# Moving attention's preparation beside the samples' columns, and the heads' sums of squares into the next unit

## The chip, the cores and the metric

The kernel runs on one core of a Trainium2 chip (trn2). The metric is the device time of one execution in microseconds. Of the kernel before there are three timed runs and one profiled execution.

## What is computed

The reference is one inference step of a hybrid decoder trunk: a prompt of 512 tokens behind 16 meta tokens, and 8 sample tokens with caches. Cut to what matters:

```python
xn = rmsnorm(x, norm_gain)
h = jnp.einsum('btd,de->bte', xn, w_in)                       # 2048 -> 16 q heads, 4 k, 4 v, z_a, u, z_s, g_a, g_s
q, k, v, z_a, u, z_s, g_a, g_s = jnp.split(h, IN_SPLITS, axis=-1)
q = rope(rmsnorm(q.reshape(b, t, 16, 64), q_norm_gain), pos)  # per head of 64
k = rope(rmsnorm(k.reshape(b, t, 4, 64), k_norm_gain), pos)
...
s = einsum(q, k) / 8                                          # window of 128, 16 meta keys, one sink per head
w = exp(s - m) / (sum(exp(s - m)) + exp(sink - m))
o = einsum(w, v)                                              # times the gate of z_a, then a 2048-wide merge
```

Beside attention stands a branch of 64 diagonal state-space groups on u, and both are merged by gates and two more products with weights. The sample tokens attend to 128 cached keys, 16 meta keys and themselves.

## The kernel before

**Columns.** The 528 prompt positions and 8 sample tokens are 536 columns, in two halves c of CH = 268; the last four columns of each half are samples. Activations have features on the partitions and columns on the free axis.

**Units.** Every weight block of 128 output rows is a unit. The fp32 weights come from HBM by SP (`raw`, L1006), ScalarE casts a high part (`whi`, L1007), VectorE subtracts it for a low part (`wlo`, L1008), three buffers each. `mm` (L1164) multiplies a unit: two weight tiles (h = 0, 1), eight k-tiles each, three products of high and low parts, two column halves, so 96 matmuls of 260 or 268 columns into one PSUM tile of the pool `mmp`, which has two buffers. VectorE frees it by the product `z<-mm` with the columns' norms R: L1194 in `evac` for gate blocks, with tanh (L1199) and L1200 behind it, and L1325 in `heads`. Later stages (L1373) form other groups of products out of the same weights.

**Order of the units.** ORDER1 writes it out by hand: "xuhuhuhuhuhuhuhuhhhhh", where x is a gate block, u an input of the state-space branch, h one of twelve head blocks: keys (0, 1), values (2, 3), queries (4 to 11). Gate blocks and later products follow.

**Head blocks.** `heads(i)` evacuates the block, stores it in DRAM twice, straight and with the halves of each head swapped (`rawD`), and squares it on ScalarE. After every odd i other than 3 four matmuls with the selector `sel` (L1343) sum the squares of two blocks per head; ScalarE copies them out (L1346), and SP stores them to `skD` (keys) or `sqD` (queries). After i = 11 `head_norms` (L1353) loads all sums back in a compact form (L1357), scales them (L1358), takes reciprocal roots by three Newton steps on VectorE (`rsqrt_dve`, L559 to L564), and stores `rkD` and `rqD` (L1360). `z` and `t` in these steps are rings of two buffers that the evacuations use as well.

**The background.** `Background` holds generators in lanes. Out of `mm`, every `grain` k-tiles, it is stepped with a budget: a generator's `yield cost` uses credit, `yield None` ends its lane's turn until the next step. `samples()` (lane 2) prepares the sample columns: loads of the heads' columns and their norms (`x<-rawD`, `x<-rkD`, `x<-rqD`, by GpSimd, L576 to L583), rope on VectorE (L588 to L593), two transposes on TensorE (L597, L598), copies (L602, L603), stores, and then the sample attention itself. `attention()` (lane 0) waits until `smp` is filled, which happens once those copies and stores of the samples are issued. Then it loads its constants (`k_attc`, L1106) and, in this order, makes the values (`vb`, `mt`, L758 to L776, with transposes on TensorE), the keys (loads `sbw<-rawD` L697 and `rb<-rkD` L701; rope L712, L713, L715; product with the norms L724; `out_k` L734; high part KH L747, low part KL L749; copies to the other partitions L752), the first q (`load_q`, then rope L712 to L715, L721, high and low parts `QT` L788, L789), and the scores (L805, L806), softmax, transposes and weighing, block by block for four kv heads. The pool of `sbw`, `sv` and `rb` has two buffers.

**What sets the order on the engines.** A tile framework places the instructions of the program by a simulated timeline and priorities; evacuations and weight splits have a high one (HIGH). On each engine the instructions then stand in a fixed row, and one that waits holds all behind it.

## Time and profile before

| | |
|---|---|
| three runs | 1272.38, 1271.10, 1270.46 us |
| median | 1271.1 us |
| profiled execution | 1273.38 us |
| its span, first to last instruction | 1271.6 us |
| mean granted TensorE clock in it | 0.995 |
| DMA traffic in it | 219.22 MB, 172 GB/s |

In the rows of the profile PE is TensorE, PEld its weight loads, DVE is VectorE, ACT ScalarE, POOL GpSimd, SP the engine that issues most DMAs; a q behind a name is its sequencer. `mm<-xh,whi` means: written is mm, read are xh and whi. A timeline row has the start, the duration, engine, line, operation, tiles, shape and count, and in brackets how long the engine had stood idle before it and what ended that. PEclk is the granted TensorE clock, 1.00 being full speed.

### The profile page before, as it was taken

The page shows a single profiled execution, that of the slowest core. Times are in us where ns is not written, and L with a number is a line of the kernel's source. Part 1 is how long each engine was busy: PE and PEld are TensorE (multiplying, and loading weights), DVE is VectorE, ACT ScalarE, POOL GpSimd, SP SyncE. Part 2 cuts the span into 40 slices and gives each one's busy share as a digit, 9 for nine tenths or more (in the row PEclk, how much of TensorE's full clock was granted, in tenths as well). Part 3 has the DMA queues.
Part 4 walks back from the last instruction along what each step waited for, and adds up shares of the span by engine and source line. Part 5 has one row for each costly group of instructions (what it writes and reads, how often), then busy time and mean ns, then how long its engine had stood idle before and what let it go on. Part 6 is the DMA issues. An engine that isn't in the chain of part 4 may idle for free.

```text
span 1271.6 us, 26531 instructions
## 1 busy us (share of the span) xinstructions
PE 1254.8 (99%) x10357; PEld 1230.1 (97%) x10357; DVE 980.0 (77%) x1554; ACT 629.2 (49%) x1344; POOL 264.2 (21%) x437
## 2 busy tenths in 40 slices
PE   9999999999999998999999998999999999999998
PEld 9999999999999998999999998999999999999998
DVE  8686888887787567888798277999976467787775
ACT  8554444454545594556523234567556333344342
POOL 0003999940000141222220133110011000000000
PEclk9999999999999998999999998999999999999999
DMA  8544343353434654555554767777666665565441
GB/s 293 203 157 157 123 142 128 123 177 129 146 109 154 223 171 138 169 164 165 152 149 129 232 170 224 220 261 222 206 196 239 195 191 183 157 204 157 146 141 51
DMA packets 108002, 219.22 MB, mean 172 GB/s; under 512 B 21933, under 2 KB 47493, under 8 KB 107845
## 3 DMA queue, kind: packets, MB, share of 16 engines
q1 hardware_dynamic: 99172, 198.53, 49.0%
q0 software_dynamic: 8704, 19.00, 5.7%
q8 instruction: 81, 1.33, 0.4%
q14 instruction: 45, 0.36, 0.1%
HBM read 181.57 MB, written 36.82 MB: 172 GB/s over the span
## 4 chain that ended last, share of the span: by engine, by line
PE 81%; DMA 7%; DVE 4%; ACT 4%; issue 2%; SPq 1%; POOL 0%; DVEq 0%; POOLq 0%; ACTq 0%
PE mm L1164 37%; PE pr L1373 35%; ACT ct L346 2%; PE wg L854 2%; DMA raw<-in_w 2%; PE aux L1373 1%; DMA c<-in_cT 1%; DVE wlo L1008 1%; DMA xr<-in_x 1%; PE aux L805 1%; ACT whi L1007 1%; DMA x<-rawD 1%; DMA bN<-in_bN 1%; PE aux L806 1%; PE mm L1680 1%
## 5 line engine op out<-in xcount | busy, mean ns | idle before, releaser
L1074 DVE TENSOR_TENSOR wlo<-raw,whi 128x1024 fp32r<-128x1024 f32 x161 | 198.7, 1256 | 69.5 <-ACT whi L1073 69.2
L1073 ACT CAST whi<-raw 128x1024 fp32r<-128x1024 f32 x161 | 166.5, 1049 | 167.7 <-DVE raw L1072 76.0
L1007 ACT CAST whi<-raw 128x1024 fp32r<-128x1024 f32 (+3 forms) x128 | 122.3, 965 | 141.6 <-PE mm L1164 95.4
L1164 PE MATMUL mm<-xh,whi 128*128 128x260 f32 (+1 forms) x792 | 186.4, 289 | 0.2 <-ACT xr L1222 0.2
L1164 PE MATMUL mm<-xl,whi 128*128 128x260 f32 (+1 forms) x792 | 184.6, 286 | 0.0
L1164 PE MATMUL mm<-xh,wlo 128*128 128x260 f32 (+1 forms) x792 | 184.6, 287 | 0.0
L1008 DVE TENSOR_TENSOR wlo<-raw,whi 128x1024 fp32r<-128x1024 f32 (+3 forms) x128 | 142.2, 1119 | 45.6 <-ACT whi L1007 44.9
L1373 PE MATMUL pr<-tau,whi 128*128 128x260 f32 x928 | 168.6, 283 | 0.0
L1373 PE MATMUL pr<-cb,whi 128*128 128x260 f32 x848 | 153.0, 283 | 0.0
L1373 PEld LDWEIGHTS pr<-tau,whi 128*128 128x128 f32 x928 | 143.0, 188 | 0.0
L1164 PEld LDWEIGHTS mm<-xh,whi 128*128 128x128 f32 x792 | 133.1, 190 | 3.4 <-issue 2.6
L1164 PEld LDWEIGHTS mm<-xl,whi 128*128 128x128 f32 x792 | 133.5, 190 | 0.8 <-issue 0.8
L1164 PEld LDWEIGHTS mm<-xh,wlo 128*128 128x128 f32 x792 | 132.4, 190 | 0.0
L1373 PEld LDWEIGHTS pr<-cb,whi 128*128 128x128 f32 x848 | 130.8, 188 | 0.2 <-ACT z L1407 0.2
L1373 PE MATMUL pr<-tau,wlo 128*128 128x260 f32 x464 | 130.8, 282 | 0.0
L1373 PE MATMUL pr<-cb,wlo 128*128 128x260 f32 x424 | 119.1, 283 | 0.2 <-DVE wlo L1074 0.2
L1072 DVE TENSOR_TENSOR raw<-raw 128x1024 f32<-128x1024 f32 x91 | 113.1, 1243 | 1.6
L1164 PE MATMUL mm<-Y,whi 128*128 128x260 f32 x576 | 104.7, 287 | 0.0
L1373 PE MATMUL pr<-xl,whi 128*128 128x260 f32 x352 | 98.9, 283 | 0.0
L1373 PE MATMUL pr<-xh,wlo 128*128 128x260 f32 x352 | 98.8, 283 | 0.0
L1373 PE MATMUL pr<-xh,whi 128*128 128x260 f32 x352 | 97.1, 283 | 0.0
L1373 PEld LDWEIGHTS pr<-tau,wlo 128*128 128x128 f32 x464 | 87.2, 188 | 0.0
(421 smaller groups left out, 2980.2 us busy)
## 6 DMA issues: line engine op xcount, KB each, us to landing
raw<-in_w SPq DMA_DIRECT2D x202, 512.0 KB, 4.6
gD<-z SPq DMA_DIRECT2D x34, 260.0 KB, 3.1
t<-gD SPq DMA_DIRECT2D x32, 260.0 KB, 2.9
cache<-in_vc POOLq DMA_DIRECT2D x16, 286.0 KB, 3.6
cache<-in_kc POOLq DMA_DIRECT2D x15, 288.0 KB, 4.1
xr<-in_x SPq DMA_DIRECT2D x16, 268.0 KB, 6.5
xg<-in_x SPq DMA_DIRECT2D x8, 536.0 KB, 4.6
sbw<-rawD SPq DMA_DIRECT2D x16, 260.0 KB, 4.3
```

Of the source, the lines that this page charges most:

```text
L346: nc.scalar.activation(out=dst, in_=src, func=AF.Copy, scale=x)
L805: nc.tensor.matmul(ps[:, e, 0:272], lhsT=q, rhs=KH[:, k0:k0 + 272], start=True, stop=False)
L806: nc.tensor.matmul(ps[:, e, 0:272], lhsT=q, rhs=KL[:, k0:k0 + 272], start=False, stop=True)
L854: nc.tensor.matmul(pv[64 * e:64 * e + 64, 0:256], lhsT=V, rhs=pr[:, e::2], start=(i == 0), stop=(i == len(parts) - 1))
L1007: nc.scalar.copy(out=hi, in_=raw)
L1008: self.dve = nc.vector.tensor_tensor(out=lo, in0=raw, in1=hi.bitcast(F32), op=ALU.subtract).ins
L1072: nc.vector.tensor_tensor(out=o, in0=o, in1=i, op=ALU.add)
L1073: nc.scalar.copy(out=hi, in_=t)
L1074: nc.vector.tensor_tensor(out=lo, in0=t, in1=hi.bitcast(F32), op=ALU.subtract)
L1164: m = nc.tensor.matmul(ps[:, c, 0:W], lhsT=wt[:, k], rhs=xo(kt, c), start=f, stop=l)
L1373: m = nc.tensor.matmul(bank, lhsT=wt[:, p], rhs=x(p, e), start=first and f and p == 0, stop=l and p == 7, skip_group_check=not first and l ...
L1680: nc.tensor.matmul(ps[:, c, 0:260], lhsT=w2[kt // 8][j][:, kt % 8], rhs=xk(xh, kt, c, 8), start=False, stop=(kt, j) == (15, 1))
```

## The change

The counts of instructions are the same on TensorE; what changes is when things are issued.

- The sums of squares of `heads` become a function that is put on a list `pend`. `mm` calls all that is on it when the first half (h = 0) of the unit's products has been issued, so the sums of a pair stand in the middle of the next unit.
- `head_norms`, the start of `samples()` and a mark in `normed` go on the same list after the last head block.
- `attention()` starts on that mark, no longer on `smp`. Its values, keys and first q no longer wait for the samples' columns.
- Before the first q's rope it passes NLOAD = 3 steps, and after it waits for `smp`, so that the first scores are issued behind the samples' transposes, copies and stores. Between the first q and its scores it passes NDELAY = 1 step, before 2.

```diff
-NDELAY = 2
+NLOAD = 3
+NDELAY = 1
...
+    pend, normed = [], []
+
     def mm(n, hi_of, lo_of, w0, budget=None, after=None, pool=None, name=None):
...
+            while pend and h == 0:
+                pend.pop(0)()
             if after:
                 after(h)
...
-        if i % 2:
+        def sums():
             if "ax" not in S:
                 S["ax"] = aux.tile([P, 2, 512], F32, name="aux")
             ps = S["ax"][:, 1, P:]
...
+        if i % 2:
+            pend.append(sums)
...
             if n == 11:
-                head_norms()
-                bg.add(samples(), lane=2)
+                pend.extend((head_norms, lambda: bg.add(samples(), lane=2), lambda: normed.append(1)))
             continue
...
-        while not smp:
+        while not normed:
             yield None
...
         for kv in range(4):
+            if kv == 0:
+                for _ in range(NLOAD):
+                    yield None
             yield from at.queries(kv)
+            while not smp:
+                yield None
             if kv == 0:
                 for _ in range(NDELAY):
                     yield None
```

Line numbers in the changed kernel are higher by 1 near the weights, by 6 from `evac` to `heads` and by 9 in `head_norms`.

**VectorE, the keys beside an evacuation.** Before, from the keys' rope on; L1194 is the evacuation `z<-mm`, L724 the keys' product with their norms `rb`, KL the low parts of the keys:

```order
L713 SCALAR_TENSOR_TENSOR sbw<-sbw,k_attc 128x536
L1200 SCALAR_TENSOR_TENSOR z<-t,z 128x520
L715 TENSOR_TENSOR sbw<-sbw 128x536
L1194 TENSOR_TENSOR z<-mm,R 128x520
L724 TENSOR_TENSOR sbw<-sbw,rb 128x536
L1008 TENSOR_TENSOR wlo<-raw,whi 128x1024
L715 TENSOR_TENSOR sbw<-sbw 128x536
L1200 SCALAR_TENSOR_TENSOR z<-t,z 128x520
L749 TENSOR_TENSOR KL_9463<-sbw,KH_9459 64x4x64 x2
```

In the changed kernel, where the evacuation is L1200:

```order
L1009 TENSOR_TENSOR wlo<-raw,whi 128x1024
L563 SCALAR_TENSOR_TENSOR t<-t,z 128x65
L724 TENSOR_TENSOR sbw<-sbw,rb 128x536
L564 SCALAR_TENSOR_TENSOR z<-t,z 128x65
L724 TENSOR_TENSOR sbw<-sbw,rb 128x536
L562 TENSOR_TENSOR t<-z 128x65
L749 TENSOR_TENSOR KL_9336<-sbw,KH_9332 64x4x64 x2
L1200 TENSOR_TENSOR z<-mm,R 128x520
L563 SCALAR_TENSOR_TENSOR t<-t,z 128x65
L749 TENSOR_TENSOR KL_9336<-sbw,KH_9332 64x4x16
```

Before, the evacuation stood ahead of both products L724 and of all KL; now both products and the first KL steps stand ahead of it.

**VectorE, the first q beside the next evacuation.** Before; the rows on `128x520` with `k_attc` are the first q's rope, which waits for the load `sbw<-rawD`, and x_9262 belongs to the samples:

```order
L592 TENSOR_TENSOR x_9262<-x_9262 128x64
L749 TENSOR_TENSOR KL_9466<-sbw,KH_9462 64x4x64 x2
L749 TENSOR_TENSOR KL_9466<-sbw,KH_9462 64x4x16
L712 SCALAR_TENSOR_TENSOR sbw<-sbw,k_attc 128x520
L713 SCALAR_TENSOR_TENSOR sbw<-sbw,k_attc 128x520
L715 TENSOR_TENSOR sbw<-sbw 128x520
L1194 TENSOR_TENSOR z<-mm,R 128x520
L721 TENSOR_TENSOR sbw<-sbw,rb 128x4x64 x2
L1008 TENSOR_TENSOR wlo<-raw,whi 128x1024
L1200 SCALAR_TENSOR_TENSOR z<-t,z 128x520
```

In the changed kernel, where x_9361 belongs to the samples:

```order
L593 COPY x_9361<-x_9361 128x16
L1206 SCALAR_TENSOR_TENSOR z<-t,z 128x520
L712 SCALAR_TENSOR_TENSOR sbw<-sbw,k_attc 128x520
L713 SCALAR_TENSOR_TENSOR sbw<-sbw,k_attc 128x520
L1200 TENSOR_TENSOR z<-mm,R 128x520
L591 TENSOR_TENSOR x_9361<-x_9361 128x64
L591 TENSOR_TENSOR x_9361<-x_9361 128x16
L712 SCALAR_TENSOR_TENSOR sbw<-sbw,k_attc 128x520
L713 SCALAR_TENSOR_TENSOR sbw<-sbw,k_attc 128x520
L1009 TENSOR_TENSOR wlo<-raw,whi 128x1024
```

Before and now one evacuation stands behind the first q's rope; now it is that of an earlier unit, the samples' steps are spread around it, and the second q's rope follows at once.

**SP, from the keys' norms to the first q's loads.** Before; rkD and rqD are the norms, `rb` their copies on all partitions, `sbw<-rawD` of 128x2x260 the loads of the first q:

```order
L1360 DMA rkD<-z 67x32
L701 DMA rb<-rkD 64x536 x2
L1006 DMA raw<-in_w 128x1024
L701 DMA rb<-rkD 64x536 x2
L1006 DMA raw<-in_w 128x1024
L1360 DMA rqD<-z 128x65
L1201 DMA gD<-z 128x520
L734 DMA out_k<-sbw 128x536
L701 DMA rb<-rqD 64x520 x2
L1006 DMA raw<-in_w 128x1024
L1201 DMA gD<-z 128x520
L697 DMA sbw<-rawD 128x2x260 x2
```

In the changed kernel:

```order
L1366 DMA z<-sqD 128x65
L1007 DMA raw<-in_w 128x1024
L1369 DMA rkD<-z 67x32
L701 DMA rb<-rkD 64x536 x4
L1007 DMA raw<-in_w 128x1024
L734 DMA out_k<-sbw 128x536 x2
L697 DMA sbw<-rawD 128x2x260 x2
L1369 DMA rqD<-z 128x65
L697 DMA sbw<-rawD 128x2x260 x2
L1007 DMA raw<-in_w 128x1024
L701 DMA rb<-rqD 64x520 x2
```

Ahead of the store of rkD a weight block now stands behind the load `z<-sqD`, the four `rb` of the keys stand together, and the first q's loads moved ahead of rqD, of a gate's store gD and of the q norms' `rb`.

## The prediction, made before the result was known

> **What bounds the kernel now.** I read the page's busy shares first, then TensorE's chain of waits, then 4-us windows around the waits. The page:

> ```profile
> PE 1254.8 (99%) x10357; PEld 1230.1 (97%) x10357; DVE 980.0 (77%) x1554; ACT 629.2 (49%) x1344; POOL 264.2 (21%) x437
> ```

> TensorE is busy for 99% of the span, so a change that adds and removes no matmul can gain only where TensorE waits, or where its clock is low. Its waits (microseconds in all, times, longest):

> ```profile
> PE aux L1343 <- DVE sst L486: 6.2, 2, 4.6
> PE aux L805 <- DVE QT L789: 3.9, 1, 3.9
> ```

> The change names both lines: L1343 is the heads' sums of squares, L805 the first scores. The windows (stretch, its length, busy time and instructions of PE, PEld, DVE, ACT, POOL, then PEclk, DMA share, GB/s) show what a wait costs beside its own length:

> ```profile
> core 0: us, PE busy (x) PEld busy (x) DVE busy (x) ACT busy (x) POOL busy (x), PEclk, DMA share, GB/s
> 500.00:504.00 4.00, 1.91 (x12) 1.06 (x12) 3.97 (x17) 1.44 (x3) 0.09 (x1) 0.68 0.00 0
> 624.00:628.00 4.00, 2.36 (x23) 1.73 (x22) 3.87 (x15) 4.00 (x17) 0.27 (x1) 1.00 0.44 131
> 628.00:632.00 4.00, 4.00 (x45) 3.66 (x44) 3.33 (x6) 1.98 (x4) 1.68 (x4) 1.00 0.42 143
> 764.00:768.00 4.00, 4.00 (x34) 3.84 (x33) 2.02 (x3) 0.00 (x0) 2.53 (x5) 1.00 1.09 310
> 768.00:772.00 4.00, 0.05 (x2) 0.01 (x1) 3.94 (x8) 2.88 (x4) 2.24 (x5) 0.89 0.82 227
> 772.00:776.00 4.00, 4.00 (x17) 3.78 (x18) 3.93 (x6) 0.40 (x1) 3.36 (x7) 0.50 0.91 259
> 776.00:780.00 4.00, 4.00 (x28) 4.00 (x28) 3.67 (x8) 2.50 (x4) 0.22 (x1) 0.76 1.07 341
> 800.00:825.00 25.00, 25.00 (x209) 24.19 (x208) 23.80 (x42) 15.36 (x39) 3.98 (x7) 1.00 0.77 227
> ```

> At 768 to 772 TensorE stands for 3.95 us. In the next 8 us the granted clock is 0.50 and then 0.76, and 17 + 28 = 45 matmuls are done where the undisturbed window at 764 does 34 in four. The missing 2 x 34 - 45 = 23, at 4.00/34 = 0.118 us each, are 2.7 us. The stall at the first scores therefore costs 3.95 + 2.7 = 6.65 us. The wait of 1.64 us (4.00 - 2.36 at 624) is followed by clock 1.00: it cost only itself. Between these two lies the length at which a wait begins to cost the clock too; I take the middle, 2.8 us.

> **The sums in the next unit.** The same matmuls, copies and stores are issued, so this edit adds no work. In the changed order of instructions the sums of heads 1, 5 and 7 stand exactly where they stood; only those of 9 and 11 move, by about half a unit, and no row shows TensorE waiting at those two. The 6.2 us of L1343 thus stay: gain 0, cost 0 for the sums themselves. What the edit does cost lies behind the last pair: the head norms now start behind later sums, and the work that hung on the samples is queued differently. That is a path of DMAs and VectorE steps, whose prices are these. SP's issues before:

> ```profile
> 735.67 0.33 SPq L1357 DMA_DIRECT2D z<-sqD  x1
> 736.12 0.25 SPq L1360 DMA_DIRECT2D rkD<-z  x1
> 738.05 1.18 SPq L701 DMA_DIRECT2D rb<-rkD  x2
> ...
> 755.09 1.27 SPq L697 DMA_DIRECT2D sbw<-rawD  x2
> ```

> The store of the norms in the chain that ended last, and three answers on DMAs (count, KB each, median us to landing): the keys' loads at 708 with nothing else under way, rb at 738, and the crowd of 750 to 760:

> ```profile
> 736.12 1.92 DMA rkD<-z
> ```

> ```profile
> sbw<-rawD SPq DMA_DIRECT2D x4, 268.0 KB, 6.7
> ```

> ```profile
> rb<-rkD SPq DMA_DIRECT2D x2, 134.0 KB, 3.3
> ```

> ```profile
> raw<-in_w SPq DMA_DIRECT2D x2, 512.0 KB, 11.8
> KH<-KH POOLq DMA_DIRECT2D x4, 144.0 KB, 8.1
> KL<-KL POOLq DMA_DIRECT2D x4, 144.0 KB, 8.2
> out_k<-sbw SPq DMA_DIRECT2D x2, 268.0 KB, 4.8
> rb<-rqD SPq DMA_DIRECT2D x4, 130.0 KB, 8.7
> ```

> VectorE's steps (start, duration, what it waited for), and ScalarE's cast that marks a unit's start:

> ```profile
> 746.80 0.22 DVE L564 SCALAR_TENSOR_TENSOR z<-t,z 128x65 f32<-128x65 f32 x1
> ...
> 749.48 0.71 DVE L724 TENSOR_TENSOR sbw<-sbw,rb 128x536 f32<-128x536 f32 x1
> ...
> 752.47 1.81 DVE L749 TENSOR_TENSOR KL<-sbw,KH 64x256 fp32r<-64x256 f32 x6
> ...
> 765.42 0.76 DVE L712 SCALAR_TENSOR_TENSOR sbw<-sbw,k_attc 128x520 f32<-128x520 f32 x1 [6.58 <-DMA sbw<-rawD]
> 766.71 0.76 DVE L713 SCALAR_TENSOR_TENSOR sbw<-sbw,k_attc 128x520 f32<-128x520 f32 x1 [0.53 <-DMA sbw<-rawD]
> 767.50 0.70 DVE L715 TENSOR_TENSOR sbw<-sbw 128x520 f32<-128x520 f32 x1
> 768.12 0.69 DVE L1194 TENSOR_TENSOR z<-mm,R 128x520 f32<-128x520 f32 x1
> 768.73 0.75 DVE L721 TENSOR_TENSOR sbw<-sbw,rb 128x256 f32<-128x256 f32 x2
> 769.40 1.22 DVE L1008 TENSOR_TENSOR wlo<-raw,whi 128x1024 fp32r<-128x1024 f32 x1
> 770.53 0.69 DVE L1200 SCALAR_TENSOR_TENSOR z<-t,z 128x520 f32<-128x520 f32 x1
> 771.25 1.41 DVE L789 TENSOR_TENSOR QT<-sbw,QT 64x512 fp32r<-64x512 f32 x2
> ```

> ```profile
> 747.57 1.05 ACT L1007 CAST whi<-raw 128x1024 fp32r<-128x1024 f32 x1 [1.69 <-issue]
> ```

> **What goes.** Before, the first q's rope (L712) got its load at 765.42, 10.3 us after its issue, and its QT came late for the first scores. Now the q load is issued earlier and the scores stand behind the samples' transposes, about 17 matmuls later. I take this stall as gone: 6.65 us.

> **What is late next: the evacuations.** A unit's PSUM is freed by VectorE's product z<-mm (L1194), and with two PSUM buffers each unit waits for the evacuation of the unit but one before. In the new order both evacuations of this stretch stand behind attention's steps that wait for a DMA, and all VectorE work behind those steps is queued too.

> *Stall A, keys.* Now rkD's last step stands behind the step that waits for z<-sqD. Issue 735.7 as before; 3.3 us to land (price of rb at 738, the nearest small load); two small steps of 0.2: 739.4. Store 1.9: 741.3. Four rb issues of 0.59, the last begun by 743.1 and done by 743.7; 3.3 us more: 746.4 to 747.0. Both key products L724 are ahead of the evacuation, then two small steps (0.4) and two KL steps (1.81/6 = 0.3 each): 0.7 + 0.4 + 0.6 + 0.7 for the evacuation = 2.4, so it ends at 748.8 to 749.4. TensorE is ready for that unit at about 747.4 (the cast at 747.57 stands at the same boundary). Stall A is 1.4 to 2.0; I take 2.0, since a wait's end also has to travel. The far end of rb is the crowd's 8.7, but the crowd comes later; that end I leave to the slower cases.

> *Stall B, the first q.* TensorE goes on at 749.4 and needs the next evacuation 96 matmuls later, 96 x 0.119 = 11.5: 760.9. It stands behind L712 and L713, which wait for the q loads. These use the buffer that out_k of the first keys frees: keys' product about 746.6, out_k 4.8, so issue at 751.4 and 752.0. Landing: 6.7 with nothing beside it, 8.7 like the crowd's rb, 10.3 like the same load before. I take 7.7, between the first two, because of the transfers queued on SP ahead of it only one out_k is then still under way, while the KH and KL copies are. So 759.1 and 759.7; 0.76 + 0.76 + 0.69: evacuation done at 761.3, stall B 0.4. Ends: 0 at 6.7, 1.4 at 8.7, 3.5 at 10.3 (with the second load 1.29 behind the first, as at 766.71).

> *Stall C, the samples' transposes.* From that evacuation to the samples' last product VectorE has 0.4 of small adds, 0.76 + 0.76, 1.22, 0.70, 0.2, 0.69, 0.70, 0.75, 0.69, 1.22, 0.75, 0.70, 0.2 = 9.7; rows overlap by some 0.08 each (768.12 to 768.73 is 0.61 for 0.69), fourteen times 1.1: 8.65. TensorE gets there after 65 matmuls, 7.75. Stall C 0.9, or about 0 when B leaves VectorE a lead.

> The sum: 2.0 + 0.4 + 0.9 = 3.3 added, none over 2.8, so no clock is lost; 6.65 removed; **3.35 gained**. The profiled execution took 1273.4 (span 1271.6) and would take 1270.0; the median of the runs is 1271.1, and from it the forecast is **1267.8**.

> [...]

> **The rivals.** *1, faster: the loads land as in an empty chip.* Loads at 6.7, stall A 1.4, B 0, C 0.2 at most: 1.4 to 1.6 added, 5.1 gained, 1266.0. For it: the q load comes some 4 us earlier than at 755.09. Against: the DMA share there was over 1, and eight KH/KL copies come at the same time. [...]

> *2, slower: the evacuation is held by a late q load.* From a landing of 9.6 us on B passes 2.8 and TensorE's clock falls as at 772: at 10.3, 2.0 + 3.5 + 2.7 + 0.9 = 9.1, 2.45 lost, 1273.6; at the 11.8 of raw (evacuation at 763.2 + 2.2 = 765.4, B 4.5) 10.1, 3.45 lost, 1274.6. For it: the same load did take 10.3. Against: it stood among more transfers then.

> *3, no change: the lead is given back.* VectorE has 23.80 of 25 us busy at 800; where TensorE comes earlier, VectorE's next evacuations can be late by as much: 1271.1. Against: TensorE waits nowhere there now, with 1.2 us to spare in 25.

> **How the numbers follow.** Forecast's own case 0.42 (landings 7.2 to 9.0, 1267.0 to 1269.1), rival 1 0.20, rival 2 0.24, rival 3 0.10, anything else 0.04. About 0.2%, 2.5 us, is what a measurement can tell from no change. Of the forecast's case 0.30 gains more than that and 0.12 less. Faster 0.30 + 0.20 + 0.01 = 0.51; same 0.12 + 0.10 + 0.01 = 0.23; slower 0.24 + 0.02 = 0.26. The range goes from rival 1 with rb at its best (1265.6) to rival 2 at 1274.6; the forecast's own is 1267.0 to 1269.1.

> **What would show it.** Right: the waits of the changed kernel still have L1343 with 6.2 us in two; L805 <- QT is gone; in its place mm <- z (evacuation) with about 2 and under 1.5 us, and a wait of the samples' transposes under 1; PEclk stays 1.00 from 745 to 785. Step A is wrong if the keys' rb land after 747.5, step B if L712 of the first q starts outside 758 to 761. The prediction is wrong if a 4-us window there shows PEclk 0.5, if L1343's waits change, or if TensorE waits anew between 780 and 1000.

## The result and the profile after

The changed kernel took 1263.7 us (median of 5 runs, 1260.33 to 1264.03), the kernel before 1270.46 us (5 runs, 1267.56 to 1272.38): ratio 0.9943, 95% interval 0.9928 to 0.9958, so 5 to 9 us faster. In a later series, with other runs of both, it was 0.9959 (0.9941 to 0.9976). The forecast was 1267.8, 3.35 us faster, with a range that began at 1265.6. The profiled execution of the changed kernel took 1264.03 us, its span is 1262.3.

TensorE's waits after (line waited at, engine and line waited for, us in all, times, longest):

```profile
PE mm L1168 <- DVE t L563: 2.9, 1, 2.9
PE tr L1216 <- DVE var L1270: 1.1, 1, 1.1
...
PE aux L1349 <- DVE sst L486: 0.6, 1, 0.6
```

The first scores (L805) have left the list, as forecast, and an evacuation (`mm` waits) has come in with 2.9 us, as forecast, if longer. (The list names L563, a small step that stands right behind the evacuation L1200 in VectorE's row; L1200 ran from 740.57 to 741.25, and TensorE went on at 741.40.) But the sums of squares (L1349, before L1343), which were to keep 6.2 us, have 0.6. The windows show the same at their two places, the sums at 496 to 504 and the evacuation at 736 to 748:

```profile
496.00:500.00 4.00, 4.00 (x36) 3.42 (x36) 3.15 (x6) 3.80 (x13) 0.56 (x1) 1.00 0.23 92
500.00:504.00 4.00, 4.00 (x44) 3.66 (x43) 4.00 (x13) 0.67 (x3) 3.83 (x8) 1.00 0.54 150
```

```profile
736.00:740.00 4.00, 2.46 (x21) 2.25 (x19) 1.73 (x5) 1.83 (x7) 0.71 (x2) 1.00 0.80 252
740.00:744.00 4.00, 2.60 (x12) 2.63 (x13) 3.91 (x14) 3.17 (x8) 2.61 (x6) 0.57 0.88 245
744.00:748.00 4.00, 4.00 (x23) 4.00 (x23) 3.46 (x10) 0.00 (x0) 0.84 (x2) 0.58 1.19 271
```

Where the time came from is read from steps that both kernels have, at the same place of the work. The product `uf<-mm` stands once behind each input of the state-space branch, `z<-pr` near the end. Before, and then after:

```profile
466.84 0.71 DVE L1573 TENSOR_TENSOR uf<-mm,R 128x536 f32<-128x536 f32 x1
...
502.91 0.70 DVE L1573 TENSOR_TENSOR uf<-mm,R 128x536 f32<-128x536 f32 x1
...
654.58 0.70 DVE L1573 TENSOR_TENSOR uf<-mm,R 128x536 f32<-128x536 f32 x1
...
1150.66 0.76 DVE L1777 SCALAR_TENSOR_TENSOR z<-pr,z 128x260 f32<-128x260 f32 x2 [0.29 <-PE pr L1373]
```

```profile
466.95 0.72 DVE L1581 TENSOR_TENSOR uf<-mm,R 128x536 f32<-128x536 f32 x1 [0.32 <-PE mm L1168]
...
496.26 0.72 DVE L1581 TENSOR_TENSOR uf<-mm,R 128x536 f32<-128x536 f32 x1 [0.20 <-PE mm L1168]
...
646.77 0.70 DVE L1581 TENSOR_TENSOR uf<-mm,R 128x536 f32<-128x536 f32 x1
...
1141.49 0.76 DVE L1790 SCALAR_TENSOR_TENSOR z<-pr,z 128x260 f32<-128x260 f32 x2
```

The difference goes from +0.1 to -6.65 us within the 36 us around the first sums, to -7.8 by 654, before any step of attention, and to -9.2 behind attention. In these two executions attention's part, which the prediction worked out, is some 1.4 us; the rest lies where the prediction had put nothing.

What stood at 498 is seen on VectorE. Before, a small step of the samples, L589 on two blocks of keys (128x16), stood alone in its row, more than 200 us ahead of its fellows, and waited there for its load; the sums' wait of TensorE is the echo of it. The step, GpSimd's issue of that load, and the sums:

```profile
498.66 0.29 DVE L589 TENSOR_SCALAR x<-x,k_smc 128x16 f32<-128x16 f32 x1 [8.24 <-DMA x<-rawD]
```

```profile
492.68 1.45 POOL L578 DMA_DIRECT2D x<-rawD  x2 [15.42 <-DMA c<-in_cT]
```

```profile
502.09 1.12 PE L1343 MATMUL aux<-t,k_sel 128*32 128x268 f32 x8 [4.57 <-DVE sst L486]
```

The sums use a PSUM tile that VectorE's L486 has to read first, and L486 stood behind L589. The list of waits names L486, the last link; the eight idle microseconds stand a few steps further up VectorE's row.

GpSimd's bracket names `c<-in_cT`, which this load does not read. It reads `rawD`, whose last stores SP issued from 484.22 to 487.64. In the run with the sums alone, below, GpSimd goes on at 491.99, while ScalarE still waits for `c` until 492.97; there at least the bracket names the wrong DMA, and the stores of `rawD` are the likelier cause.

In the changed kernel L589 stands at 746, among the samples' other steps, where its load has long landed:

```profile
746.26 0.29 DVE L589 TENSOR_SCALAR x<-x,k_smc 128x16 f32<-128x16 f32 x1
```

The code has the reason: a background step is queued behind the latest weight split on VectorE (`bg.after = (ws.dve,) if at is not None else ()`) only once attention exists. Before, the samples' steps ran ahead of attention and were not held; the framework placed the one whose inputs were written early as early as it could. After, attention exists when they run.

### The profile page after: what moved, and what is told of

Its sections match the earlier page's. It is cut to its first block, busy times and chain, and to the rows that moved or that the text cites. A ratio compares the mean times of both kernels' runs of the same rounds, so it can differ in the third digit from the quotient of the medians.

```text
span 1262.3 us, 26537 instructions
## 1 busy us (share of the span) xinstructions
PE 1250.9 (99%) x10357; PEld 1227.7 (97%) x10357; DVE 980.6 (78%) x1554; ACT 628.7 (50%) x1344; POOL 266.1 (21%) x437
## 4 chain that ended last, share of the span: by engine, by line
PE 92%; DVE 3%; DMA 2%; ACT 1%; SPq 1%; issue 0%; DVEq 0%; ACTq 0%
PE mm L1168 45%; PE pr L1382 35%; PE wg L854 2%; PE mm L1255 2%; PE aux L1382 1%; PE aux L1168 1%; PE aux L1255 1%; DVE wlo L1009 1%; PE aux L806 1%; PE aux L805 1%; ACT ct L346 1%; PE tr L526 1%; PE tr L836 1%; PE wg L526 1%; DMA Y<-yD 0%
## 5 line engine op out<-in xcount | busy, mean ns | idle before, releaser
L1008 ACT CAST whi<-raw 128x1024 fp32r<-128x1024 f32 (+3 forms) x128 | 122.3, 965 | 132.3 <-PE mm L1168 85.6
## 6 DMA issues: line engine op xcount, KB each, us to landing
raw<-in_w SPq DMA_DIRECT2D x202, 512.0 KB, 4.3
xr<-in_x SPq DMA_DIRECT2D x16, 268.0 KB, 6.5
```

What stands on the lines that cost most here:

```text
L1008: nc.scalar.copy(out=hi, in_=raw)
```

## The experiments

Theory A: the unforeseen part of the gain is that step's leaving its early place on VectorE. Rival B: all of the gain is attention's preparation beside the samples. Rival C: it is the sums' place in the next unit.

**The kernel before with the step queued behind the weight split.** The edit, which holds for the samples' products on swapped halves and for nothing else:

```diff
-        v.tensor_scalar(out=sw[:, bl], in0=sw[:, bl], ...)
+        with split():                         # tc.issue_after(ws.dve)
+            v.tensor_scalar(out=sw[:, bl], in0=sw[:, bl], ...)
```

> The kernel before with one edit: the samples' small product on the keys' two blocks (L589, 128x16), which stood alone at 498 us in VectorE's row and waited 8.24 us there for its load, is queued behind the latest weight split, so that it stands at 734 us beside the samples' other steps. Nothing of the change is in it. Theory A (the 6 us of the sums' waits came from this step, not from where the sums stand): the wait of 4.57 us at L1343 and the low clock behind it go, the wait of 1.64 us at 626 may shrink, the first scores' wait of 3.9 us stays; 6 to 7.5 us faster, ratio 0.994 to 0.995. Theory B (the gain of the change comes from attention's preparation beside the samples): within 1 us of before. Theory C (it comes from the sums' place in the next unit): within 1 us of before.

It took 1267.77 us against 1271.19, ratio 0.9974 (0.9960 to 0.9989): 3.3 us faster, about half of what A expected, more than B and C allow. Its waits, and the window at the second sums:

```profile
PE aux L806 <- DVE QT L790: 4.2, 2, 4.0
PE aux L1344 <- DVE sst L486: 2.1, 1, 2.1
```

```profile
620.00:624.00 4.00, 1.93 (x13) 0.97 (x12) 3.69 (x15) 4.00 (x16) 0.45 (x1) 0.76 0.41 131
624.00:628.00 4.00, 4.00 (x39) 3.67 (x38) 3.51 (x7) 0.67 (x3) 1.68 (x4) 0.81 0.51 156
```

The long wait at 498 is gone, the first scores' is not. The second sums waited 2.1 us here, and their wait was 0.6 to 2.1 us in all the profiles, with the step in its early place or not: that one is not the step's. It was 1.6 to 2.1 us in the four profiles in which attention waits for the samples, and 0.6 to 1.4 in the eight in which it does not, so the change shortens it too. By what was not tried.

**The changed kernel with the step put back.** `free` switches the queueing off for this one product.

```diff
-                        for ins in self.after:
+                        for ins in (() if self.free else self.after):
...
+    free(True)
+    yield 0.0
+    swapped(slice(0, 2), 2)
+    free(False)
+    yield 0.0
```

> The changed kernel with that one step taken out of the queue behind the weight splits, so that it stands again at row 388 of VectorE, where it stood before; the sums and attention are as in the change. Theory A: the wait of some 4.5 us at L1343 (near 498 us) comes back with its low clock, and 6 to 7 us of the gain are lost: within 1.5 us of the kernel before, ratio 0.999 to 1.001. Theories B and C: as the changed kernel, ratio 0.994.

Ratio 0.9977 (0.9959 to 0.9995), 1268.5 us against 1271.19: the gain of the change falls from 5 to 7 us to 2.9, between what A and what B and C expected. Its interval, 0.6 to 5.2 us, overlaps that of the change in the later series, 3.1 to 7.5, so the size of the loss is rough. Runs spread from 1262.68 to 1272.77, and the profiled one, the fastest, shows why the sizes of A did not come out. Its step and its sums:

```profile
495.17 0.29 DVE L589 TENSOR_SCALAR x<-x,k_smc 128x16 f32<-128x16 f32 x1 [4.33 <-DMA x<-rawD]
```

```profile
498.61 0.66 PE L1359 MATMUL aux<-t,k_sel 128*32 128x268 f32 x8 [0.66 <-DVE sst L486]
```

The step waited 4.33 us there and TensorE 0.66, not 8.24 and 4.57. TensorE's wait is the step's less 3.7 us in both. So what the early step costs differs from execution to execution with the landing of its load.

**The sums alone, and attention alone.**

```diff
-        while not normed:
+        while not smp:
...
-NLOAD = 3
-NDELAY = 1
+NLOAD = 0
+NDELAY = 2
```

> Only the sums, head norms and start of the samples in the next unit; attention waits for the samples as before, with the delays as before. The samples' step stands at row 388 of VectorE as before. Theory A: L1343 keeps its waits of 4.6 and 1.6 us; within 2 us of before. Theory C: L1343's waits go, 6 to 8 us faster. Theory B: no gain.

1271.44 us against 1271.19, ratio 1.0004 (0.9989 to 1.0018). C falls: the sums' new place alone gains nothing. The step is in its early place and waits 6.04 us, the sums 2.36, again 3.7 less:

```profile
500.28 0.93 PE L1349 MATMUL aux<-t,k_sel 128*32 128x268 f32 x8 [2.36 <-DVE sst L486]
```

```diff
-                pend.extend((head_norms, lambda: bg.add(samples(), lane=2), lambda: normed.append(1)))
+                head_norms()
+                bg.add(samples(), lane=2)
+                normed.append(1)
...
-            pend.append(sums)
+            sums()
```

> Only attention beside the samples, its first scores behind them; the sums, head norms and start of the samples stand in the unit's end as before. The samples' step stands beside the others at row 825 of VectorE, and the evacuation of the gate block stands ahead of both keys' products with their norms (in the changed kernel behind both). Theory A: L1343's long wait goes (6 to 7 us), and stall A of the changed kernel (2.94 us and a low clock behind it, some 5 us) isn't there either, so it is faster than the changed kernel: 10 to 12 us under before, ratio 0.990 to 0.992. Theory B: as the changed kernel, 0.994. Theory C: no gain.

1272.47 us, ratio 1.0018 (1.0004 to 1.0031): no gain, where A expected 10 to 12 us. L1349 had no wait over 1.3 us, and the evacuation of stall A did not wait, both as expected; but a new wait took all of it, at the samples' transposes:

```profile
762.82 0.42 PE L597 MATMUL aux<-k_idn,x 128*64 128x128 f32 x1 [8.42 <-DVE x L592]
```

```profile
756.79 0.76 DVE L712 SCALAR_TENSOR_TENSOR sbw<-sbw,k_attc 128x520 f32<-128x520 f32 x1 [5.93 <-DMA sbw<-rawD]
...
762.55 0.22 DVE L592 TENSOR_TENSOR x<-x 128x64 f32<-128x64 f32 x1
```

Here the samples' last product (L592) stands behind the ropes of both q on VectorE, the first of which waits for its loads, and the transposes stand 38 rows earlier on TensorE than in the change. So neither part of the change gains anything alone. Attention beside the samples moves the step and the first q. What the later start of the norms and samples adds is more than the place of the transposes, as the run with the transposes later shows, below.

**The change again, and stall A taken out of it.** Theory A1: stall A is the evacuation standing behind the second keys' product, which waits for its load. A2: VectorE would be late with it in any case.

> The changed kernel itself, beside the next three and on the same chip, since single runs of one kernel differ by up to 8 us here and the variants are to be compared with it. All theories: ratio about 0.994 to 0.996 to the kernel before. If low clock behind a wait of 2 to 3 us is a matter of when the wait falls, its profile may show stall A (evacuation behind the keys' products, 2.5 to 3 us) with or without 0.5 of clock behind it.

1265.21 us against 1271.75, ratio 0.9959 (0.9941 to 0.9976). In its profile stall A has 2.80 us with clock 1.00 behind it, where the first profile had 2.94 us and 0.57; the transposes waited 1.30 us.

```diff
-            v.tensor_tensor(out=sb, in0=sb, in1=rb, op=ALU.mult)
+            with self.freed():                    # tc.issue_after(latest z<-mm)
+                v.tensor_tensor(out=sb, in0=sb, in1=rb, op=ALU.mult)
```

> The changed kernel with one edit: the keys' products with their norms are queued on VectorE behind the latest evacuation that the program has written, which puts the second of the two (not the first) behind the evacuation of stall A. Theory A1 (stall A is the evacuation waiting in the row behind the second product, which waits for its load): the wait mm <- VectorE of 2.9 us falls to 0.3 to 0.8 us, its low clock goes; 2 to 5 us less than the changed kernel. Theory A2 (the evacuation would be late in any case, since VectorE has too much to do there): the same wait, no gain. A risk under A1: the samples' transposes stand some 18 rows earlier here, and may wait up to 1.5 us for the samples' last product, which takes that much back.

1269.2 us, ratio 0.9985 (0.9972 to 0.9999). A1 is right on the wait, which fell to 0.52 us, and wrong on the gain: it is 4 us slower than the change in the same series. TensorE waits 1.51 us at 868 for ScalarE's `t` (L1714). The transposes wait 4.05 us, and VectorE's row says for what, the second q's load:

```profile
763.53 0.30 PE L597 MATMUL aux<-k_idn,x 128*64 128x128 f32 x1 [4.05 <-DVE x L592]
```

```profile
760.64 0.76 DVE L712 SCALAR_TENSOR_TENSOR sbw<-sbw,k_attc 128x520 f32<-128x520 f32 x1 [5.24 <-DMA sbw<-rawD]
...
763.26 0.21 DVE L592 TENSOR_TENSOR x<-x 128x64 f32<-128x64 f32 x1
```

The next run also asks for the transposes four background steps later:

```diff
-    yield None
+    for _ in range(5):
+        yield None
     with later():
         nc.tensor.transpose(out=ps[0:64, 0:128], ...)
```

> As the one before, and the samples' transposes are asked for four background steps later, so that they stand at row 4626 of TensorE, near their place in the change (4622). Theory A1: no wait over 1 us is left between 735 and 770; 3 to 5.5 us less than the changed kernel. Theory A2: no gain.

1269.25 us, ratio 0.9982 (0.9966 to 0.9998): no gain over the last, though stall A has 0.67 us and the transposes 0.46. The wait moved 240 us on. The first scores start at 774.71 instead of 766.49, and ScalarE's casts of attention's output A, which ended 8 us ahead of the first product with A in the change, now come after it is due. That the later scores make the casts late is argued from the order of the work, not tried. The cast and the product in the change, then here:

```profile
991.65 4.33 ACT L1655 CAST A<-oT 128x520 fp32r<-128x520 f32 x8 [4.11 <-DVE oT L924]
```

```profile
1003.89 0.64 PE L1168 MATMUL mm<-A,whi 128*128 128x260 f32 x4
```

```profile
1006.52 4.31 ACT L1658 CAST A<-oT 128x520 fp32r<-128x520 f32 x8 [0.90 <-DVE oT L926]
```

```profile
1007.24 1.92 PE L1170 MATMUL mm<-A,whi 128*128 128x260 f32 x6 [2.36 <-ACT A L1658]
```

**Attention alone, with the transposes later.** The same edit, six steps, on the run with attention alone.

> Attention alone as in the run with the sums left in their place, but the samples' transposes asked for six background steps later (row 4629 of TensorE instead of 4584, some 45 rows or 7 us). That run's loss came from one wait of 8.42 us at these transposes and the low clock behind it. If that is all that the sums' place in the next unit saves, the wait falls to 0 to 1.5 us and the kernel is 8 to 11 us under that run, about 1262 to 1264; the first scores stand some 60 rows later than in the change, and if attention's end is short of time, part of it comes back as a wait near 1000 us or later (A's splits).

1273.2 us, ratio 1.0015 (1.0002 to 1.0027). The wait of 8.42 us is gone from the list, and nothing is gained: a weight split is 2.05 us late at 760, and the first product with A waits 2.02 us. The expectation that the one wait was all of it is refuted. VectorE still stands for the first q's load, and the weight split stands behind it:

```profile
756.13 0.76 DVE L713 SCALAR_TENSOR_TENSOR sbw<-sbw,k_attc 128x520 f32<-128x520 f32 x1 [6.96 <-DMA sbw<-rawD]
```

In both runs with attention alone SP issues that load behind the copies of the q norms (`rb<-rqD`), here at 745.24; in the change it stands ahead of them, at 742.48. So the later start of the norms also lets the first q's loads pass these copies; whether that is all it adds was not tried.

**The second q behind the samples.** On the run with the keys' second product behind the evacuation, both halves of the second q's rope (L712, L713) are queued behind the samples' last product with the same kind of edit.

> As the run with the keys' second product behind the evacuation, and the second q's rope (both halves) is queued on VectorE behind the samples' last product, which stood behind it and its load there: VectorE idled 5.24 us for that load with the samples' product in the row behind, and TensorE waited 4.05 us for it. Theory: the wait of the samples' transposes falls to 0 to 1 us with its low clock, stall A stays under 0.8 us; 3 to 6 us under that run, 1263 to 1266, and 0 to 3 us under the changed kernel. Rival (a moved step only passes the wait on): the first scores or a later evacuation wait for 2 us or more instead, and it is within 1.5 us of the run with the second product behind the evacuation.

1264.94 us, ratio 0.9944 (0.9925 to 0.9963): against that run's 0.9985 some 5 us less, as the theory expected, and no different from the change (0.9943 and 0.9959). Stall A and the transposes:

```profile
740.48 0.36 PE L1172 MATMUL mm<-xh,whi 128*128 128x260 f32 x1 [0.32 <-DVE t L563]
...
758.28 0.30 PE L599 MATMUL aux<-k_idn,x 128*64 128x128 f32 x1 [2.49 <-DVE x L592]
```

The transposes still wait 2.49 us, where 0 to 1 was expected. Of the change's 2.80 + 1.30 us 2.81 are left; then the second q's scores wait 0.95 and an evacuation at 866 0.97. What was taken out came back in parts. No version here clearly beats the change.

**The kernel before again.**

> The kernel before once more, for a second profile. Theory A: the samples' step at row 388 of VectorE again waits for its load, between 4 and 8.3 us as the load lands sooner or later, and TensorE's wait at L1343 near 498 us is that wait less some 3.7 us (8.24 and 4.57 in the first profile, 6.04 and 2.4, 4.33 and 0.66 in the two kernels that had the step at the same row).

One run, 1270.04 us. The step waited 4.78 us and the sums 1.11, as A said (4.78 - 3.7 = 1.1):

```profile
495.24 0.29 DVE L589 TENSOR_SCALAR x<-x,k_smc 128x16 f32<-128x16 f32 x1 [4.78 <-DMA x<-rawD]
```

## Why the prediction was wrong, point by point

**The step that failed** is "The 6.2 us of L1343 thus stay: gain 0, cost 0 for the sums themselves". It was drawn from TensorE's row alone, in which the sums of heads 1, 5 and 7 do stand where they stood. But the wait was for VectorE, and there one instruction of the samples had gone from 498.66 to 746.26 us, behind the L486 that frees the sums' tile instead of ahead of it. The waits of VectorE before, which the prediction does not use, name it in one line:

```profile
DVE x L589 <- DMA x<-rawD: 8.5, 2, 8.2
```

What the step is worth: 3.3 us (0.9974, 0.9960 to 0.9989) where it alone is moved. Put back into the change, it takes the ratio from 0.9943 or 0.9959 to 0.9977, 2 to 4 us by the medians. The 6.65 us between the two first profiles are an execution with the longest wait seen against one with none. That the step causes the wait is shown by both experiments and by every profile: the stretch between the first two products `uf<-mm` above took 29.3 us in all eight profiles without the early step, and 36.07, 34.14, 32.93 and 32.48 us in the four with it. That the load's landing sets the size is shown by those four (waits of the step of 8.24, 6.04, 4.78, 4.33 us give 4.57, 2.36, 1.11, 0.66 at the sums). Why the issue of that load comes at 490.40 in one execution of the kernel before and at 492.68 in the other was not tried.

**The first scores' stall gone, 6.65 us:** right; neither profile of the change has a wait at L805.

**Stall A, 1.4 to 2.0 us:** the mechanism was right, as the experiment with the product behind the evacuation shows; it measured 2.94 and 2.80. Two terms were too small, the store of the keys' norms and the landing of their copies `rb`:

```profile
730.29 0.26 SPq L1369 DMA_DIRECT2D rkD<-z  x1
733.10 2.46 SPq L701 DMA_DIRECT2D rb<-rkD  x4
```

```profile
737.04 0.72 DVE L724 TENSOR_TENSOR sbw<-sbw,rb 128x536 f32<-128x536 f32 x1 [1.12 <-DMA rb<-rkD]
...
739.13 0.72 DVE L724 TENSOR_TENSOR sbw<-sbw,rb 128x536 f32<-128x536 f32 x1 [1.23 <-DMA rb<-rkD]
```

The prediction took 1.9 us for the store; here the first issue of `rb`, which reads it, came 2.81 us behind the store's. The prediction took 3.3 us from the last issue of `rb` to its landing; here the last of the four began at 735.0, and the second product started at 739.13, at the end of a wait for `rb`, 4.1 us later. The way of a wait's end to TensorE, for which the prediction took the upper of its two values, is 0.15 us here (741.25 to 741.40).

**Stall B, 0.4 us:** 0. The first q's load landed about 5.2 us after its issue (742.48 to 747.73), under the prediction's lowest row of 6.7, and the evacuation at 749.20 held nobody. That row was misread as the price of an idle time: SP had issued `k_attc`, `sv` and a weight block in the 2.1 us ahead of those loads. (Also, 96 x 0.119 is 11.4, not 11.5.)

```profile
742.48 1.24 SPq L697 DMA_DIRECT2D sbw<-rawD  x2
```

```profile
747.73 0.76 DVE L712 SCALAR_TENSOR_TENSOR sbw<-sbw,k_attc 128x520 f32<-128x520 f32 x1 [0.50 <-DMA sbw<-rawD]
748.41 0.76 DVE L713 SCALAR_TENSOR_TENSOR sbw<-sbw,k_attc 128x520 f32<-128x520 f32 x1
749.20 0.70 DVE L1200 TENSOR_TENSOR z<-mm,R 128x520 f32<-128x520 f32 x1
```

Rival 2, a late load, did not happen in the change; its mechanism did, in the variants above.

**Stall C, 0.9 us:** 0 in one profile of the change, 1.30 in the other.

**No clock lost under 2.8 us:** wrong as a rule. In the first profile of the change the clock fell to 0.57 behind 2.94 us, in the second it stayed at 1.00 behind 2.80. Elsewhere 2.07 and 2.36 us lost it, and 2.49 us did not. The last section has what the traces show of this.

**The sum for attention, 3.35 us gained:** right in size. With the step put back the change gains 2.9 us (0.6 to 5.2). In the profiles the stretch from the last product `uf<-mm` to `z<-pr` (654.58 to 1150.66 before) took 496.08 and 496.48 us in the two of the kernel before, 494.72 and 492.89 in the two of the change and 491.38 with the step put back, so 1.4 to 5.1 us less. That the middle of this fits is partly luck, since the terms did not come out one by one: stall A was longer, stall B nothing, and the clock fell in one execution of three.

**The rivals:** rival 1 gave nearly the measured time, 1266.0, by luck: loads were quick for the first q, but stall A was longer, not shorter, and about half of the gain came from the step. Rival 3, the lead given back by VectorE at 800, is not seen; TensorE is busy throughout from 788 to 800.

**Its signs of being wrong:** three came up. L1343's waits changed, a window behind stall A shows a clock of 0.57, and the first q's rope started at 747.73, some 755.5 on the time scale of the kernel before, which ran 7.8 us later there; the prediction gave 758 to 761.

## What to carry to other kernels

A wait belongs to the row of the engine that is waited for: before a stall is called untouched, compare that engine's row too, and read its own list of waits for an instruction that sits there for a DMA. A step that a scheduler places far ahead of its fellows, because its inputs are written early, holds all behind it until its load lands, here for 4.33 to 8.24 us; queue it behind something that is certainly later. Where one wait ends just ahead of the next, taking it out moves it: here 2.8 us at an evacuation came back at the transposes, at attention's output, or in small parts.

## What the runs showed of the hardware that was not expected

A wait's length alone did not decide whether TensorE's clock fell behind it: 2.07 us (the step behind the split; clock 0.76 and 0.81 in the windows at 620 and 624), 2.36 us (the sums alone; 0.57 at 500 to 504) and 2.94 us (the change; 0.57 and 0.58 at 740 and 744) lost it, while 2.49 us (the second q behind the samples) and 2.80 us (the change again) left it at 1.00.

```profile
767.68:771.10 3.42, 0.36 (x4) 0.16 (x2) 3.42 (x6) 2.15 (x4) 1.82 (x5) 1.00 0.84 235
771.10:774.51 3.41, 2.52 (x10) 2.30 (x11) 3.28 (x6) 1.14 (x2) 2.58 (x5) 0.50 0.81 191
774.51:777.92 3.41, 3.41 (x18) 3.41 (x18) 3.14 (x7) 0.93 (x2) 1.71 (x4) 0.50 1.06 358
```

```profile
737.12:740.54 3.42, 1.34 (x12) 1.14 (x10) 2.19 (x6) 2.37 (x9) 1.06 (x2) 1.00 0.88 282
740.54:743.95 3.41, 2.55 (x12) 2.58 (x13) 3.32 (x13) 2.63 (x7) 2.21 (x5) 0.50 0.91 247
743.95:747.36 3.41, 3.41 (x17) 3.41 (x17) 3.25 (x10) 0.00 (x0) 0.89 (x2) 0.50 1.15 272
```

```profile
738.73:742.14 3.41, 2.30 (x20) 2.09 (x18) 1.44 (x3) 1.71 (x6) 0.54 (x1) 1.00 0.80 249
742.14:745.55 3.41, 1.73 (x14) 1.76 (x15) 3.35 (x12) 3.20 (x8) 2.36 (x5) 1.00 0.90 273
```

```profile
618.70:622.11 3.41, 1.44 (x12) 1.23 (x11) 3.14 (x9) 3.41 (x15) 0.00 (x0) 1.00 0.26 60
622.11:625.52 3.41, 3.31 (x18) 2.50 (x19) 2.72 (x9) 2.55 (x8) 0.56 (x1) 0.50 0.43 174
```

So the same wait can cost the clock in one execution and not in the next, as stall A did (0.57 behind 2.94 us, 1.00 behind 2.80); the raster's place differs from execution to execution, with a boundary at 740.54 in the first profile of the change and at 742.14 in the second.

The kernel before ran between 1266.01 and 1274.71 us in 35 runs on one chip. Its two profiles differ by 3.5 us in the step's wait alone (8.24 and 4.78), so one profile of it is a sample, and a term read from its longest wait, 6.65 us here, can be too large for the median, 3.3 us.
